# Taking the embedding's product out of the gate: two hybrid decoder layers on one Trainium2 core

## The chip, the core and the metric

The kernel runs on one core of a Trainium2 chip. The core has TensorE (PE, with its weight loads PEld), VectorE (DVE), ScalarE (ACT), GpSimd (POOL) and SyncE (SP, which issues most DMAs). TensorE reads from SBUF and writes to PSUM, which has eight banks of 128 x 512 f32. The metric is device microseconds of one execution: the median over runs of the same program. All inputs, weights and outputs lie in DRAM when an execution begins and ends.

## The reference

Two layers, 512 tokens, width 1024. All arithmetic is f32.

```python
def hybrid_layer(x, p_i, positions, w_in, ...):
    h = x @ w_in                                  # q, k, v of two head groups, and an indexer
    oa = swa_sink_attention(qa, ka, va, sinks)    # window of 128 keys, with sinks
    ob = dsa_sparse_attention(qb, kb, vb, qi, ki, wi, k_top)   # 128 best keys by the indexer's score
    mix = jnp.concatenate([oa, ob], axis=-1) @ w_o
    x = layer_norm(DN_ALPHA * x + mix, ln1_g, ln1_b)
    g, u = jnp.split(x @ w_gu, 2, axis=-1)
    ffn = (jax.nn.silu(g) * u) @ w_down
    ple = (p_i @ w_pp) * jax.nn.sigmoid(x @ w_pg)
    return layer_norm(DN_ALPHA * x + ffn + ple, ln2_g, ln2_b)
```

The change is about `ple`. Its factor `p_i @ w_pp` (512 x 256 by 256 x 1024) depends on two inputs of the kernel alone, and not on `x`; it is called the embedding's product below. The other factor, `sigmoid(x @ w_pg)`, is the gate.

## The kernel before

The tokens lie in four tiles of 128 (`t` = 0 to 3); `xt[t]` holds the residual stream of one tile. For products the stream is turned to features by `to_features` (line 406) into `fh` and `fl`, the high and the low part of each value. Every product of that kind is three matmuls, `mm3` (line 314): high by high, high by low, low by high. The matmuls of nearly all products therefore bear the lines 316 to 318, and they are told apart by their tiles.

A weight goes through a queue written out ahead (`wq`, line 163, filled by `plan`). `w_dma` loads a block of 512 KB into one of three staging buffers `wst` by SP; `w_split` turns it into a high part (ACT, line 269) and a low part (POOL, line 270) in one of five buffers `wsp`. A block marked `extra` goes to `slot` buffers instead, by ACT (line 263) and DVE (line 264). `w_take` hands a block to a product, `w_rel` gives the buffer back and starts the next split. There are 28 buffers `slot` and 12 buffers `t2k` of 128 x 512. All PSUM tiles come from one pool of eight banks.

The stages of a layer, in the order of the program:

- `start()` (line 791): `project` multiplies tile by tile with the indexer's columns, 296 wide (`gi_out`, line 518, normalizes and rotates the indexer's keys and queries on DVE, with parts on ACT and POOL; its `turns` transpose them later), then with the keys' and values' columns, 384 wide (`kv_out`, line 559), in two blocks of two tiles, then the first queries.
- `index()` (line 610) runs interleaved with it, by the costs that a small planner (`Order`, line 42) adds up: for `t` = 1 to 3 it waits until the turned keys and queries are there, and then issues eight score matmuls (line 617) of 128 to 512 columns, each with a relu on ACT (line 619) and a weighted sum on DVE (line 620). `topk()` (line 625) follows on DVE.
- `rest()`, `attention()` and `topk()` interleaved; then `last_o()` (line 822), the last part of the output projection, by single tiles. The norm behind the attention, `ln_sums` (line 395), starts for a tile when its last half is there; DVE does most of it (lines 402 and 404).
- `gate_up(True, ...)` (line 831) begins the feed-forward part: `to_features(0)`, `to_features(1)`, products of the first 256 tokens, `to_features(2)`, `to_features(3)`. The feed-forward part is six groups (`GROUPS`, line 178). In the group after the first, `p` (loaded in line 959) is transposed in lines 947 to 955 and kept as `pT` in four `slot` buffers.
- The gate (lines 979 to 1020): for each of the four tiles and each half `h` of the 1024 columns, 24 matmuls of 512 columns with `w_pg` into the bank `ps`, then six with `w_pp` into the bank `pq` (line 997). ACT takes the sigmoid of `ps` (line 1002), DVE multiplies by `pq` (line 1003) and adds to the stream (line 1012, in the second layer 1005), and the second norm follows. The blocks of the second half are `extra`. At the end of the first layer `to_features` and the next `start()` follow; at the end of the second the output is stored.

Tile builds each engine's queue from the program. It keeps the order of what depends on one another, but may issue later work earlier on an engine where an earlier instruction is not ready by its own model of time.

## Time and profile before

| | us |
|---|---|
| time, median of 3 runs (1295.0 to 1297.23) | 1295.97 |
| profiled execution, its own time | 1295.42 |
| its span in the trace | 1293.6 |
| PE busy | 1244.4 (96%) |
| DVE busy | 837.7 (65%) |
| POOL busy | 666.8 (52%) |
| ACT busy | 575.7 (44%) |

The page gives busy time by engine, the span in 40 slices, the DMA queues and the chain of work that ended last: 81% of that chain is PE's, 12% DVE's. The stages lie so in the span: first layer to 653.7 us (indexer and attention to 241.9, feed-forward part to 596.8, gate to 653.7), second layer behind it (attention to 873.5, feed-forward part to 1228.5, gate to 1283.4, the last norm and store to 1293.6). The timelines and the table by stretches show each engine in such a stage; a matmul's duration there is modelled and overlaps the next one's, so that start to start is the measure of its cost.

### The profile page before, as it was taken

How to read it: one execution, taken by the hardware profiler on the slowest of the kernel's cores; microseconds unless marked ns; L12 is line 12 of the kernel's file. 1: busy time of each engine (PE TensorE's matmuls, PEld its weight loads, DVE VectorE, ACT ScalarE, POOL GpSimd, SP SyncE). 2: the span in 40 equal slices, each digit the busy share in tenths (PEclk: the TensorE clock that was granted, in tenths of full speed). 3: DMA queues.
4: the chain of work that ended last, by engine and by line, in shares of the span. 5: the costliest groups of instructions: out<-in, count | busy, mean ns of one | idle time of the engine just before them, and what ended most of it. 6: DMA issues, size and time to landing. Idle time of an engine off the chain costs nothing.

```text
span 1293.6 us, 18329 instructions
## 1 busy us (share of the span) xinstructions
PE 1244.4 (96%) x6632; PEld 1073.3 (83%) x6632; DVE 837.7 (65%) x1866; ACT 575.7 (44%) x1216; POOL 666.8 (52%) x477
## 2 busy tenths in 40 slices
PE   6799999899999999999998999998999999999996
PEld 4799889788888888888897997888888888888885
DVE  8899965864545453635679997765827273636276
ACT  2656765343343433333337576744434343434220
POOL 7565432357475757563155544414665665757422
PEclk9799999999999999999998999999999999999998
DMA  5133121332232424134032313103342414231321
GB/s 171 50 98 99 58 74 33 98 109 92 94 114 82 129 67 131 33 114 136 2 97 70 111 34 98 50 17 128 101 126 70 139 59 145 67 113 34 114 82 49
DMA packets 89123, 112.77 MB, mean 87 GB/s; under 512 B 5444, under 2 KB 65860, under 8 KB 89032
## 3 DMA queue, kind: packets, MB, share of 16 engines
q1 hardware_dynamic: 88360, 111.58, 27.8%
q8 instruction: 52, 0.85, 0.3%
q14 instruction: 39, 0.32, 0.1%
q10 hardware_dynamic: 672, 0.03, 0.0%
HBM read 109.49 MB, written 2.10 MB: 86 GB/s over the span
## 4 chain that ended last, share of the span: by engine, by line
PE 81%; DVE 12%; ACT 2%; issue 2%; DMA 1%; POOL 1%; DVEq 0%; SPq 0%; POOLq 0%; ACTq 0%
PE bank L316 24%; PE bank L317 24%; PE bank L318 24%; PE bank L656 2%; PE bank L700 2%; DVE t2k L476 2%; PE bank L694 2%; DVE work L620 1%; DVE m L631 1%; DVE work L632 1%; DVE t2k L474 1%; DMA wst<-in_w_pg_dram 1%; DVE x L404 1%; POOL wsp L270 1%; PE bank L486 1%
## 5 line engine op out<-in xcount | busy, mean ns | idle before, releaser
L270 POOL TENSOR_TENSOR wsp<-wst,wsp 128x1024 fp32r<-128x1024 f32 (+2 forms) x148 | 353.4, 2402 | 273.4 <-ACT wsp L269 271.2
L317 PE MATMUL bank<-fl,wsp 128*128 128x512 f32 (+1 forms) x768 | 284.9, 372 | 2.0 <-DVE fl L415 2.0
L316 PE MATMUL bank<-fh,wsp 128*128 128x512 f32 (+1 forms) x768 | 283.6, 372 | 1.0 <-ACT fh L414 1.0
L318 PE MATMUL bank<-fh,wsp 128*128 128x512 f32 (+1 forms) x768 | 283.2, 371 | 0.0
L269 ACT CAST wsp<-wst 128x1024 fp32r<-128x1024 f32 (+2 forms) x148 | 151.3, 1032 | 158.3 <-PE bank L318 108.1
L843 DVE TENSOR_TENSOR t2k<-bank,t2k 128x512 f32<-128x512 f32 x44 | 30.4, 692 | 222.2 <-PE bank L318 222.2
L317 PEld LDWEIGHTS bank<-fl,wsp 128*128 128x128 f32 x768 | 144.7, 188 | 27.4 <-DVE fl L415 2.4
L316 PE MATMUL bank<-wsp,fh 128*128 128x256 f32 (+3 forms) x512 | 165.9, 326 | 0.7 <-ACT fh L414 0.3
L318 PE MATMUL bank<-wsp,fl 128*128 128x256 f32 (+3 forms) x512 | 164.6, 323 | 1.5 <-DVE fl L415 1.5
L316 PEld LDWEIGHTS bank<-fh,wsp 128*128 128x128 f32 x768 | 143.6, 188 | 26.6 <-ACT fh L414 1.9
L318 PEld LDWEIGHTS bank<-fh,wsp 128*128 128x128 f32 x768 | 144.7, 188 | 24.9
L317 PE MATMUL bank<-wsp,fh 128*128 128x256 f32 (+3 forms) x512 | 164.4, 321 | 0.0
L248 POOL TENSOR_TENSOR wsp<-slot,wsp 128x512 fp32r<-128x512 f32 x100 | 141.5, 1439 | 28.5 <-ACT wsp L247 28.5
L316 PE MATMUL bank<-wsp,slot 128*128 128x512 f32 x392 | 153.5, 392 | 0.0
L317 PE MATMUL bank<-wsp,slot 128*128 128x512 f32 x392 | 152.7, 390 | 0.0
L775 DVE TENSOR_TENSOR x<-bank,x 128x512 f32<-128x512 f32 x140 | 91.5, 686 | 88.5 <-PE bank L318 88.5
L318 PE MATMUL bank<-wsp,slot 128*128 128x512 f32 x392 | 148.4, 389 | 0.0
L875 ACT CAST slot<-t2k 128x256 fp32r<-128x256 f32 (+1 forms) x104 | 49.8, 497 | 144.1 <-DVE t2k L843 102.5
L248 POOL TENSOR_TENSOR wsp<-t2k,wsp 128x512 fp32r<-128x512 f32 x40 | 57.5, 1448 | 93.0 <-ACT wsp L247 93.0
L316 PEld LDWEIGHTS bank<-wsp,fh 128*128 128x128 f32 x512 | 98.3, 192 | 7.5 <-ACT fh L414 1.0
L318 PEld LDWEIGHTS bank<-wsp,fl 128*128 128x128 f32 x512 | 97.9, 192 | 7.1 <-DVE fl L415 2.1
L317 PEld LDWEIGHTS bank<-wsp,fh 128*128 128x128 f32 x512 | 98.4, 192 | 5.4
(166 smaller groups left out, 2189.4 us busy)
## 6 DMA issues: line engine op xcount, KB each, us to landing
wst<-in_w_gu_dram SPq DMA_DIRECT2D x88, 512.0 KB, 3.5
slot<-in_w_down_dram SPq DMA_DIRECT2D x80, 256.0 KB, 2.8
wst<-in_w_in_dram SPq DMA_DIRECT2D x16, 512.0 KB, 3.6
wst<-in_w_o_dram SPq DMA_DIRECT2D x16, 512.0 KB, 3.7
wst<-in_w_pg_dram SPq DMA_DIRECT2D x16, 512.0 KB, 4.0
wst<-in_w_in_dram SPq DMA_DIRECT2D x8, 256.0 KB, 2.8
lng<-in_ln_g_dram SPq DMA_DIRECT2D x4, 512.0 KB, 6.3
lnb<-in_ln_b_dram SPq DMA_DIRECT2D x4, 512.0 KB, 6.3
```

Of the source, the lines that this page charges most:

```text
L248: G.tensor_tensor(w[:, 1, j], src[j], w[:, 0, j], OP.subtract)
L269: A.copy(w[:, 0, :a * n], st[:, :a * n])
L270: G.tensor_tensor(w[:, 1, :a * n], st[:, :a * n], w[:, 0, :a * n], OP.subtract)
L316: PE.matmul(o, sh, mh, start=start, stop=False, skip_group_check=again)
L317: PE.matmul(o, sh, ml, start=False, stop=False, skip_group_check=again)
L318: PE.matmul(o, sl, mh, start=False, stop=stop, skip_group_check=again)
L476: V.tensor_tensor(t1.rearrange("p n (u i) -> p n u i", u=2), t1.rearrange("p n (u i) -> p n u i", u=2), t2.rearrange("p n (u i) -> p n u i ...
L656: PE.matmul(ps[:, o:o + nn], qT[kind, t, g][:, j * 128:(j + 1) * 128], kT[c, s][:, k0:k0 + nn], start=(s == 0), stop=(s == 1))
L694: PE.matmul(o, vt[b0 + b][:, f:f + 128], pts[b][:, u], start=b == 0 and u == 0, stop=b == nb - 1 and u == 1)
L775: V.tensor_tensor(xt[t][:, c], ps, xt[t][:, c], OP.add)
L843: V.tensor_tensor(a, ps[1, f], a, OP.mult)
L875: A.copy(h[0], src)
```

## The change

The embedding's product leaves the gate. Its first half of columns is computed in `index()`, ahead of the first score matmuls of tile 1; the second half in the first `gate_up`, two tiles behind `to_features(0)` and two behind `to_features(1)`. `p` is no longer loaded into `slot` buffers: a new entry of the weight queue, "stage", loads it into a staging buffer (512 KB), twice a layer, and `embed_parts` transposes and splits it, twice a layer, into four `t2k` buffers. `embed` makes six matmuls for a tile, ACT copies the bank to a `t2k` buffer and issues a DMA that writes it to a tile in DRAM. `w_pp` takes a `wsp` buffer each time, between the keys' weights and the queries', and between the output projection's and the feed-forward part's. In the gate, SP loads the eight pieces back (256 KB each) into `slot` buffers, and the multiplication of line 1003 reads them there and not in PSUM.

```diff
--- before.py
+++ after.py
@@ -97,6 +97,7 @@
     slots = ctx.enter_context(tc.tile_pool(name="slots", bufs=NSLOT))
     tmp = ctx.enter_context(tc.tile_pool(name="tmp", bufs=NTMP))
     small = ctx.enter_context(tc.tile_pool(name="small", bufs=4))
+    dram = ctx.enter_context(tc.tile_pool(name="dram", bufs=1, space=bass.MemoryType.DRAM))
     psum = ctx.enter_context(tc.tile_pool(name="psum", bufs=1, space=bass.MemoryType.PSUM))
 
     order = Order()
@@ -169,6 +170,11 @@
     def rows(w, k, a, c0, c1):
         return w[k * 128:(k + a) * 128, c0:c1]
 
+    def plan_embed(l, h):
+
+        wq.append(("stage", (p[l, 0],), None))
+        plan(2, rows(w_pp[l], 0, 2, h * 512, (h + 1) * 512))
+
     def plan_down(w, f):
 
         wq.append(("raw", w, f))
@@ -181,6 +187,7 @@
             plan(a, rows(w_in[l], k, a, QI, NIN))
         for k in range(0, KT, 2):
             plan(2, rows(w_in[l], k, 2, KA, KA + 256), rows(w_in[l], k, 2, KB, KB + 128))
+        plan_embed(l, 0)
         for c in (QA, QA + 256, QB, QB + 256):
             for k in range(0, KT, 4):
                 plan(4, rows(w_in[l], k, 4, c, c + 256))
@@ -188,6 +195,7 @@
             for h in range(2):
                 for k in range(k0, k0 + 4, 2):
                     plan(2, rows(w_o[l], k, 2, h * 512, (h + 1) * 512))
+        plan_embed(l, 1)
         for fs in GROUPS:
             for f in fs:
                 for c in (f * 256, FF + f * 256):
@@ -201,7 +209,6 @@
         for h in range(2):
             for k in range(0, KT, 2):
                 plan(2, rows(w_pg[l], k, 2, h * 512, (h + 1) * 512), extra=h == 1)
-            plan(2, rows(w_pp[l], 0, 2, h * 512, (h + 1) * 512), extra=h == 1)
 
     wst_live, w_live = {}, {}
     W_AHEAD, ST_AHEAD = 5, 3
@@ -223,6 +230,7 @@
                     SP.dma_start(quarter[q][j], w[r:r + 128, h * 512:(h + 1) * 512])
             return
         a, cols, _ = wq[i]
+        a = 4 if a == "stage" else a
         n = sum(ap.shape[1] for ap in cols)
         st = wst.tile([128, 1024], F32, name="wst", tag="wst")
         sv = st[:, :a * n].rearrange("p (a n) -> p a n", a=a)
@@ -236,7 +244,7 @@
 
     def w_split(i):
 
-        if wq[i][0] == "raw":
+        if wq[i][0] in ("raw", "stage"):
             return
         if wq[i][0] == "op":
             src = quarter[wq[i][1]]
@@ -292,7 +300,7 @@
                 wpos["dma"] += 1
                 go = True
             i = wpos["split"]
-            if i < wpos["dma"] and (wpos["room"] or wq[i][0] == "raw" or wq[i][2] is True and wq[i][0] != "op"):
+            if i < wpos["dma"] and (wpos["room"] or wq[i][0] in ("raw", "stage") or wq[i][2] is True and wq[i][0] != "op"):
                 w_split(i)
                 wpos["split"] += 1
                 go = True
@@ -306,6 +314,12 @@
         wpos["use"] = i + 1
         assert i in w_live, (i, wpos)
         return w_live.pop(i)
+
+    def stage_take():
+        i = wpos["use"]
+        wpos["use"] += 1
+        assert wq[i][0] == "stage" and i < wpos["split"], i
+        return wst_live.pop(i)
 
     def w_rel():
         wpos["room"] += 1
@@ -514,6 +528,7 @@
         qiT, qT, work, wi, vt, vb, ma = {}, {}, {}, {}, {}, {}, {}
         ready = set()
         kin, kmv = {}, {}
+        pe, first_half = {}, []
 
         def gi_out(t, ps):
 
@@ -607,9 +622,36 @@
                 yield None
 
 
+        def embed_parts():
+            st = stage_take()
+            parts = []
+            for k in range(2):
+                ps = bank("tp", 2)
+                for t in range(NT):
+                    PE.transpose(ps[:, tok(t)], st[:, t * 256 + k * 128:t * 256 + (k + 1) * 128], idf)
+                parts.append([t2k(F32R), t2k(F32R)])
+                A.copy(parts[k][0], ps)
+                V.tensor_tensor(parts[k][1], ps, parts[k][0], OP.subtract)
+            return parts
+
+        def embed(t, h, parts, w):
+            ps = acc()
+            for k in range(2):
+                mm3(ps, parts[k][0][:, tok(t)], parts[k][1][:, tok(t)], w[0][k], w[1][k], k == 0, k == 1)
+            a = t2k()
+            A.copy(a, ps)
+            pe[t, h] = dram.tile([128, 512], F32, name=f"pe{t}{h}", tag=f"pe{t}{h}")
+            A.dma_start(pe[t, h], a)
+
+
         def index():
             for t in range(1, NT):
                 yield from wait(("i", t), *[("ki", b) for b in range(0, t + 1, 2)])
+                if t == 1:
+                    for u in range(NT):
+                        embed(u, 0, *first_half)
+                    w_rel()
+                    yield 5.4
                 nk = (t + 1) * 128
                 work[t] = const.tile([128, nk], F32, name=f"work{t}", tag=f"work{t}")
                 for h in range(IH):
@@ -798,6 +840,7 @@
                     ln_in(t + 1)
                 yield from project(ws, 296, (t,), from_f, gi_out, 3 * (t == 3))
             ws = take(4)
+            first_half.extend([embed_parts(), w_take()])
             for b in ALL:
                 yield from project(ws, 384, b, from_f, kv_out, 4 * (b is ALL[-1]))
             for q in QS[:NSTART]:
@@ -818,6 +861,7 @@
         order.run((rest(), R_MAIN), (attention(), 1.0), (topk(), R_TOP))
         order.flush()
         wo = [take(2), take(2)]
+        second_half = embed_parts(), w_take()
 
         def last_o():
             for b in TAIL:
@@ -845,7 +889,12 @@
 
             if first:
                 to_features(0)
+                for t in range(2):
+                    embed(t, 1, *second_half)
                 to_features(1)
+                for t in range(2, NT):
+                    embed(t, 1, *second_half)
+                w_rel()
                 for j in range(2):
                     ps[j, 0], ps[j, 1] = acc(), acc()
                     for k in range(KT):
@@ -943,21 +992,6 @@
                         w_sums(hs[0]["end"])
                 else:
                     gate_up(False, lambda f, a: hs.append(parts(a)[0]))
-                if gi == 1 and f == fs[0]:
-                    pT = {}
-                    for k in range(2):
-                        ps = bank("tp", 2)
-                        for t in range(NT):
-                            o = t % 2 * 256 + k * 128
-                            PE.transpose(ps[:, tok(t)], pin[t // 2][:, o:o + 128], idf)
-                        pT[k] = [slot(), slot()]
-                        A.copy(pT[k][0], ps)
-                        V.tensor_tensor(pT[k][1], ps, pT[k][0], OP.subtract)
-            if gi == 0:
-                pin = [slot(F32), slot(F32)]
-                for i in range(2):
-                    SP.dma_start(pin[i].rearrange("p (t n) -> p t n", t=2),
-                                 p[l, 0, i * 256:(i + 1) * 256].rearrange("(t p) n -> p t n", p=128))
             if len(fs) == 2:
                 down(hs, gi == 0)
                 continue
@@ -976,31 +1010,29 @@
                     res_out(h, None)(t, ps[t])
 
 
-        wg = [take(5) if h == 0 else None for h in range(2)]
+        wg = [take(4) if h == 0 else None for h in range(2)]
+        for t in range(NT):
+            for h in range(2):
+                e = slot(F32)
+                SP.dma_start(e, pe[t, h])
+                pe[t, h] = e
         for b in TAIL:
             for h in range(2):
                 if wg[h] is None:
-                    wg[h] = take(5)
+                    wg[h] = take(4)
                 ws = wg[h]
                 c = slice(h * 512, (h + 1) * 512)
                 ps = [acc() for _ in b]
-                pq = [bank("sc", 2) for _ in b]
                 for k in range(KT):
                     w = ws[k // 2]
                     for i, t in enumerate(b):
                         mm3(ps[i], *from_f(t, k), w[0][k % 2], w[1][k % 2], k == 0, k == KT - 1)
                     if b is TAIL[-1] and h == 0 and k % 2 == 1:
                         w_rel()
-                for k in range(2):
-                    w = ws[4]
-                    for i, t in enumerate(b):
-                        mm3(pq[i], pT[k][0][:, tok(t)], pT[k][1][:, tok(t)], w[0][k], w[1][k], k == 0, k == 1)
-                if b is TAIL[-1] and h == 0:
-                    w_rel()
                 for i, t in enumerate(b):
                     a = t2k()
                     A.activation(a, ps[i], AF.Sigmoid)
-                    V.tensor_tensor(a, pq[i], a, OP.mult)
+                    V.tensor_tensor(a, pe[t, h], a, OP.mult)
                     if l == L - 1:
                         V.tensor_tensor(xt[t][:, c], xt[t][:, c], a, OP.add)
                         ln_stats(t, h)
```

## Rows read from the trace of the kernel before

**Rows 1.** By stretch, us: busy PE, PEld, DVE, ACT, POOL (counts), clock, DMA, GB/s

```profile
53.53:66.94 13.41, 12.17 (x44) 9.92 (x45) 11.37 (x34) 10.48 (x32) 3.17 (x8) 0.50 0.01 2
...
105.00:160.00 55.00, 52.94 (x409) 49.97 (x407) 54.49 (x194) 41.37 (x127) 23.81 (x26) 1.00 0.28 86
...
596.80:653.70 56.90, 56.76 (x260) 46.88 (x259) 37.16 (x75) 21.99 (x39) 14.64 (x7) 1.00 0.27 81
...
684.18:691.80 7.62, 7.51 (x32) 6.10 (x32) 5.76 (x14) 6.88 (x20) 1.45 (x5) 0.51 0.02 4
...
691.80:736.00 44.20, 42.47 (x333) 41.80 (x333) 43.72 (x114) 26.07 (x74) 29.06 (x27) 1.00 0.28 84
```

**Rows 2.** PE's matmuls by operands, second layer's gate: count, busy us and mean ns

```profile
L316 PE MATMUL bank<-wsp,slot 128*128 128x512 f32 x8 | 3.1, 389 | 0.0
...
L318 PE MATMUL bank<-slot 128*128 128x512 f32 x8 | 3.1, 389 | 0.0
```

**Rows 3.** Timeline of PE, end of the last gate: start, length us, instruction

```profile
1278.67 0.39 PE L317 MATMUL bank<-slot,fh 128*128 128x512 f32 x1
...
1282.97 0.39 PE L318 MATMUL bank<-slot 128*128 128x512 f32 x1
```

**Rows 4.** Timelines of ACT and DVE at the same place

```profile
1282.04 0.60 ACT L1002 ACTIVATE t2k<-bank 128x512 f32<-128x512 f32 x1 [6.20 <-PE bank L318]
...
1283.47 0.69 DVE L1003 TENSOR_TENSOR t2k<-bank,t2k 128x512 f32<-128x512 f32 x1 [4.35 <-PE bank L318]
```

**Rows 5.** PE ahead of the first scores, both layers; [idle before <- releaser]

```profile
46.81 0.96 PE L486 MATMUL bank<-idr,slot 128*128 128x128 f32 x10
...
53.53 2.73 PE L617 MATMUL bank<-slot 128*128 128x256 f32 x8 [5.75 <-ACT slot L487]
...
684.18 2.73 PE L617 MATMUL bank<-slot 128*128 128x256 f32 x8 [5.89 <-ACT slot L487]
```

**Rows 6.** Timelines of DVE and ACT there, first layer

```profile
52.30 0.42 DVE L474 TENSOR_TENSOR t2k<-bank,tab 128x256 f32<-128x256 f32 x1
...
61.31 0.61 DVE L474 TENSOR_TENSOR t2k<-bank,tab 128x128 f32<-128x128 f32 x2
...
52.42 0.30 ACT L479 CAST slot<-t2k 128x128 fp32r<-128x128 f32 x1 [4.07 <-DVE t2k L476]
...
52.62 1.34 ACT L487 CAST slot<-bank 128x256 fp32r<-128x256 f32 x3
```

**Rows 7.** Timeline of PE at the norm behind the attention, first layer, then second

```profile
243.65 1.09 PE L412 MATMUL bank<-idf,x 128*128 128x128 f32 x8 [1.71 <-DVE x L404]
...
246.48 0.39 PE L317 MATMUL bank<-fl,wsp 128*128 128x256 f32 x1 [0.99 <-DVE fl L415]
...
252.65 1.09 PE L412 MATMUL bank<-idf,x 128*128 128x128 f32 x8 [0.39 <-DVE x L404]
...
875.40 1.09 PE L412 MATMUL bank<-idf,x 128*128 128x128 f32 x8 [1.71 <-DVE x L404]
```

**Rows 8.** Timelines of SP's issues and of PE, first layer's gate

```profile
587.02 0.37 SPq L231 DMA_DIRECT2D wst<-in_w_pp_dram  x1
...
589.74 11.56 SPq L231 DMA_DIRECT2D wst<-in_w_pg_dram  x4
...
608.23 0.50 PE L317 MATMUL bank<-slot,fh 128*128 128x512 f32 x1
```

**Rows 9.** Timeline of DVE, end of the first layer's gate; POOL splits until 653.96

```profile
648.50 0.68 DVE L1003 TENSOR_TENSOR t2k<-bank,t2k 128x512 f32<-128x512 f32 x1
...
649.21 1.25 DVE L1012 CUSTOM_DVE_ANT_0 x<-x,t2k 128x512 f32<-128x512 f32 x1
...
654.44 0.69 DVE L1012 CUSTOM_DVE_ANT_0 x<-x,t2k 128x512 f32<-128x512 f32 x1
```

**Rows 10.** Prices of DMAs: timeline of ACT's queue, then issues by line

```profile
1.18 0.53 ACTq L151 DMA_DIRECT2D invf<-in_inv_freq_dram  x1
...
slot<-in_w_down_dram SPq DMA_DIRECT2D x80, 256.0 KB, 2.8
```

## The prediction

> **What bounds the kernel now.** I read the chain of work that ended last first: four fifths of it are TensorE's. Then the table by stretches, for where PE is not full, and the waits and timelines of those places. In the gate PE is busy for 56.76 of 56.90 us, in the second layer alike, so that a matmul taken from there should shorten the time by what it costs [rows 1]. There are two kinds of places where PE stands still. Ahead of the first score matmuls it waits 5.75 us in the first layer and 5.89 in the second, both times for ACT's copy of the turned keys [rows 5]; behind the pause it runs at half its clock, at a granted clock of 0.50 for 13.41 us and of 0.51 for 7.62 [rows 1]. At the norm behind the attention it waits 1.71, 0.99 and 0.39 us for DVE, together 3.09, and the first of these returns in the second layer at the same size [rows 7]. In the attention itself neither engine has room: from 105 to 160 us DVE is busy for 54.49 of 55 us and PE for 52.94, and from 691.8 to 736 DVE for 43.72 of 44.20 [rows 1]. The sum below is therefore made by stage: gate, first pause, norm.
>
> **The gate.** There are six groups of eight matmuls of the embedding's product for a layer, of which the first and the last are shown; that is 48 a layer [rows 2]. From the start of the matmul at 1278.67 to that at 1282.97 are 4.30 us for 19 matmuls, 0.226 each [rows 3]. 96 of them are 21.7 us that leave a full engine. At the very end a little comes back: the last six matmuls hide the sigmoid. ACT begins it at 1282.04, right behind the last product with w_pg, it takes 0.60, and the multiplication follows only at 1283.47, when the six are through [rows 4]. Without them it could start at about 1282.74, 0.73 earlier, where the six cost 1.36: +0.63. The multiplication keeps its length of 0.69 [rows 4]. In the first layer the next layer's projections stand behind the gate on PE; I count no such end there.
>
> Does PE get its weights that much earlier? Before, the block of w_pp is loaded at 587.02 between the two halves of w_pg, and the four blocks of the second half are issued over 11.56 us from 589.74; only one matmul is held visibly, 0.50 us long instead of 0.39, at 608.23 [rows 8]. PE now comes to the second half 1.36 us earlier, but the block that was loaded in front of it is gone, and each of the four moves up by one staging buffer, which is more than 1.36 us. I take nothing for it. SP gets eight loads of 256 KB behind w_pg's. Such a load takes 2.8 us to land [rows 10], its first reader is DVE behind a whole column of matmuls, and eight banks let PE go on; nothing, unless they are issued in front of w_pg's blocks. Those four took 11.56 us of SP's time for the same number of bytes [rows 8], so that loads in front of them could make them late by as much; I hold at most about 5 us a layer to show. In the feed-forward part two small loads, four slot buffers and the transposes go; the eight transposes return in the output projection's last part, full as well, and the other eight lie in the first pause: net nothing.
>
> **The norm.** Half of the product, 24 matmuls, is 5.43 us a layer. It stands where PE waits 3.09 us; its inputs have been ready long before. The first two tiles' matmuls (2.7 us) begin in the wait of 1.71 [rows 7], and push the next transposes back by about 1; the other two fill the wait of 0.99 and, being late by then, the wait of 0.39. What stays is 5.43 - 3.09 = 2.34 a layer, 4.7 for both. Bounds: nothing of it hidden, 10.9; better than 4.7 only if DVE's part ended earlier, which nothing here makes it do. ACT's four copies and four DMA issues lie beside DVE's chain. w_pp now holds a fifth wsp buffer, so that the first block of the feed-forward part is split about when its neighbours are; it is wanted 5 us later than before.
>
> **The first pause.** The other 5.43 us are as long as the pause of 5.75 or 5.89 [rows 5]. Three things decide how much fits. (1) Banks: each tile wants one of eight. When the ten transposes end (46.81 + 0.96), three banks wait for ACT's three copies at 52.62, and the two of the keys' product are held by DVE, which reads one at 52.30 and one at 61.31 [rows 5, 6]. Three tiles can go at once, 4.1 us; the fourth waits until about 53.1, and the first score follows at about 54.5 and not at 53.53: one microsecond late, for DVE too, which is full from there on. (2) ACT: four copies of about 0.6, by the sigmoid of the same size [rows 4], and four DMA issues, 0.53 by the only kind on ACT's queue [rows 10]: 4.5 us. ACT stands idle for 4.07 us up to 52.42, held by one instruction that waits for DVE [rows 6]; behind it, it is busy for 10.48 of 13.41 us [rows 1]. Copies that are queued behind the held instruction delay scores, those ahead of it cost nothing. (3) The transposed p wants two subtractions on DVE, 1.4 us by the 0.69 of one such read from a bank [rows 4], and four of twelve t2k buffers. Against these stands the clock: without a long pause it may not fall. The half clock can give back no more than what DVE leaves: 13.41 - 11.37 = 2.04 us in the first layer and 7.62 - 5.76 = 1.86 in the second [rows 1]. So the bounds for a layer are -2 and +6.8 (5.43 not hidden, and 1.4 on DVE). I take +1, the late fourth tile, with the clock's gain set against ACT and DVE: +2 for both layers.
>
> The sum: 1293.6 - 21.7 + 0.6 + 4.7 + 2.0 = 1279.2 us of span. The profiled execution took 1.8 us more than its span, and the median of the runs lies 0.55 above that execution: 1281.6, forecast 1281.5.
>
> **Rivals.** First, the moved half stays out of the pause: the block of w_pp comes late, or copies line up on ACT, and both layers pay near 6.8 instead of 1. For it: DVE and ACT are nearly full behind the pause, and a delay there meets DVE's top-k work. Against it: three banks are free. 1281.5 + 11.6 = 1293. Second, the gate does not shrink as the matmuls do, since the loads from DRAM are issued ahead of w_pg's second half: 5 us a layer, 1291.5. Against it: w_pg stands in front in the program. A third runs through DVE. The multiplication reads its factor from a bank now and from SBUF afterwards. At 648.50, while POOL is splitting, line 1003 with one operand in a bank takes 0.68, and line 1012 with both operands in SBUF takes 1.25 at 649.21, against 0.69 at 654.44 with POOL idle [rows 9]. If all sixteen multiplications paid that 0.56 and the chain went through DVE, the time would be 1281.5 + 9 = 1290.5. It doesn't by DVE's load, 37.16 of 56.90 us in the gate [rows 1], so that I give it little. The Trainium skill, page "SBUF — State Buffer", section "Who interferes with whom", has the rule for it: a VectorE instruction with two SBUF inputs contends with a GpSimd instruction that reads SBUF, and one with at most one doesn't. The rows at 648.50 and 649.21 agree with it, and it speaks against this part of the change.
>
> The rival on the other side is slower than before: t2k buffers. Tile may issue work early, and the transposes for the second half depend on nothing but a load. If their four buffers are taken before the attention's last units have theirs, these have eight of twelve. A unit over tile 3 keeps four for its exponentials, and three units are under way at a time, so that from there on one unit less overlaps. PE then waits once for each of the four units of the last two tiles in each layer. The price of one is the pause that a late step leaves, between the 1.71 of a DVE step and the 5.75 of a whole chain [rows 5, 7]; at 3 each it is 8 x 3 = 24 us, 1305. It decides as soon as the parts are made before the last unit's scores; that the output projection's last part precedes them in the program speaks against it.
>
> A better case: the clock stays up, and ACT's hole takes the copies: -2 a layer, 1275.5.
>
> **How the numbers follow.** The forecast with its neighbourhood, 1277 to 1286: 0.56. The first rival, in part or whole, 0.14; the gate's two together 0.11 (the one by DVE 0.03 of it); the better case 0.06; slower by the t2k buffers or the like 0.08; and 0.05 lies between the first rival with an unhidden norm and no change. The range of 8 in 10 goes from 1274.5 to 1292.0: it takes in the better case and most of the first two rivals. 0.2%, 2.6 us, is about what a measurement of this kernel tells from no change: faster by more 0.86, within 0.05, slower by more 0.09.
>
> **What would show it.** In the gate 192 matmuls of w_pg a layer and no others, PE full, the stage 10.9 us shorter in each layer: right. PE waiting for ACT or DVE slots there: the second rival. Ahead of the first scores, 24 matmuls where the pause was, what is left of it under 2 us, a granted clock of 1.00 behind it, and the first score one microsecond later behind the keys' copies. If it is 5 later, or if DVE has new idle time between 53 and 160 us, I was wrong by the first rival. At the norm the first feed-forward products start 2.3 us later than before, seen from the output projection's last matmul. PE idle in the attention's last tiles beside a wait for t2k: the slower rival. The prediction is wrong as a whole if attention, from the first score to the norm, grows by more than the gate gave.

## The result, and the profile after

The changed kernel takes 1304.42 us (median of 4 runs, 1304.17 to 1306.88) where the kernel before takes 1295.79 beside it; the ratio is 1.0070, 95% interval 1.0052 to 1.0087. It is slower by 0.7%, and 23 us above the forecast of 1281.5. One run of those below, of `e17_bank`, took 1355.79 with its core in a slower state, and its median leaves it out.

First the page of the changed kernel: busy time of each engine, and the clock granted to TensorE in 40 slices.

```profile
span 1305.1 us, 18472 instructions
...
PE 1252.3 (96%) x6648; PEld 1082.5 (83%) x6648; DVE 842.4 (65%) x1866; ACT 584.1 (45%) x1234; POOL 673.4 (52%) x479
...
PEclk9999999999999999999997999998999999999998
```

PE has 7.9 us more busy time than before (1244.4), of which the 16 transposes that it makes more are about 1.8, at 0.11 from start to start; the span is 11.5 longer. So some of the loss is slower matmuls, and the rest is waits. The profiled execution of the changed kernel took 1306.88, the longest of its four. 1.8 of that come in the first 31 us and belong to this execution: in `e3_pin`, whose program is the same up to there, they are 0.0.

The next table divides both spans at events that each program has once: the start of PE's transposes (line 412 before, 426 after), of the first feed-forward product over all 512 tokens, and of the first gate product. A change of length is the difference of the two differences.

| stage, up to | before, us | after, us | change of length | forecast |
|---|---|---|---|---|
| start, to tile 2's first transposes | 28.81 | 30.60 | +1.79 | 0 |
| layer 1 attention, to the norm's transposes | 240.90 | 246.61 | +3.92 | +1.0 |
| norm, to the products over 512 tokens | 272.68 | 285.42 | +7.03 | +2.34 |
| feed-forward, to the first gate product | 596.82 | 608.67 | -0.89 | 0 |
| gate, to tile 3's transposes | 664.14 | 670.29 | -5.70 | -10.86 |
| layer 2 attention | 872.65 | 887.75 | +8.95 | +1.0 |
| norm | 904.43 | 927.32 | +7.79 | +2.34 |
| feed-forward | 1228.58 | 1250.57 | -0.90 | 0 |
| gate, norm and store, to the end | 1293.6 | 1305.1 | -10.5 | -10.23 |

The second gate does what was forecast: in its stretch PE is full (columns as in [rows 1]), and by operands it runs 192 matmuls, all with w_pg.

```profile
1250.57:1294.26 43.69, 43.69 (x193) 35.85 (x191) 35.19 (x70) 7.50 (x12) 12.00 (x7) 1.00 0.27 96
```

The first gate gives back half of it. The feed-forward parts are 0.9 shorter by the eight transposes that left them. Both norms and both attentions cost far more than forecast. Now these places, in rows.

Timeline of PE ahead of the first scores, both layers (start, length, instruction, idle time before it and its releaser); these answer to [rows 5].

```profile
48.67 0.97 PE L500 MATMUL bank<-idr,slot 128*128 128x128 f32 x10
...
53.28 0.50 PE L330 MATMUL bank<-wsp,t2k 128*128 128x512 f32 x1 [2.64 <-DVE t2k L634]
...
61.37 0.75 PE L659 MATMUL bank<-slot 128*128 128x256 f32 x5
...
689.67 0.79 PE L332 MATMUL bank<-wsp,t2k 128*128 128x512 f32 x1 [3.44 <-DVE t2k L634]
...
696.95 0.85 PE L659 MATMUL bank<-slot 128*128 128x256 f32 x4
```

The product is in the pause, but it waits there itself, for the low parts of p (line 634). DVE makes them last, behind the whole rotation of the indexer's keys, and ACT's four copies and stores stand ahead of the scores' relus:

```profile
52.55 1.28 DVE L634 TENSOR_TENSOR t2k<-bank,t2k 128x512 fp32r<-128x512 f32 x2
...
63.69 0.48 DVE L662 SCALAR_TENSOR_TENSOR work<-bank,wi,causal 128x256 f32<-128x256 f32 x1 [9.20 <-ACT bank L661]
...
58.10 0.59 ACT L642 COPY t2k<-bank 128x512 f32<-128x512 f32 x1 [1.73 <-PE bank L332]
58.72 0.34 ACTq L644 DMA_DIRECT2D pe<-t2k  x1
...
61.85 0.59 ACT L642 COPY t2k<-bank 128x512 f32<-128x512 f32 x1 [0.77 <-PE bank L659]
62.33 1.05 ACT L277 CAST wsp<-wst 128x1024 fp32r<-128x1024 f32 x1
...
63.28 0.92 ACT L661 ACTIVATE bank<-bank 128x256 f32<-128x256 f32 x3
```

The first score is 7.84 us late (6.05 without the start), and DVE idles 9.20 us. The clock falls all the same: by the table of stretches (columns as in [rows 1]) it is 0.70 from 61.40 to 70.00, and 0.50 for 9 us behind the second layer's first scores.

```profile
700.00:709.00 9.00, 8.18 (x26) 7.24 (x27) 8.11 (x26) 5.81 (x22) 4.30 (x9) 0.50 0.21 58
```

At the norm, timelines of PE, then ACT, then DVE; PE's rows answer to [rows 7].

```profile
250.22 1.04 PE L426 MATMUL bank<-idf,x 128*128 128x128 f32 x8
...
254.77 0.50 PE L330 MATMUL bank<-fh,wsp 128*128 128x256 f32 x2 [0.75 <-ACT fh L428]
258.38 1.09 PE L426 MATMUL bank<-idf,x 128*128 128x128 f32 x8 [3.10 <-DVE x L418]
...
252.24 1.05 ACT L642 COPY t2k<-bank 128x512 f32<-128x512 f32 x2
...
253.18 1.05 ACT L277 CAST wsp<-wst 128x1024 fp32r<-128x1024 f32 x1
...
254.13 1.08 ACT L428 CAST fh<-bank 128x512 fp32r<-128x512 f32 x2
...
255.62 2.70 DVE L418 SCALAR_TENSOR_TENSOR x<-x,lns,lnb 128x1024 f32<-128x1024 f32 x1
258.43 1.27 DVE L429 TENSOR_TENSOR fl<-bank,fh 128x512 fp32r<-128x512 f32 x2
```

The old waits of 1.71 and 0.99 are filled, as forecast. But tile 1's transposes are done at 251.3, and ACT copies their result only at 254.13, behind two copies of the product and a split; DVE's low part of it (258.43) then falls behind a step of the norm. Tile 2's transposes stand behind two feed-forward matmuls on PE, where they stood behind 48: Tile planned them there. PE waits 3.10.

At the end of the first gate, PE, DVE and POOL:

```profile
658.03 1.25 PE L426 MATMUL bank<-idf,x 128*128 128x128 f32 x8 [3.91 <-DVE x L418]
...
650.37 2.20 DVE L1035 TENSOR_TENSOR t2k<-slot,t2k 128x512 f32<-128x512 f32 x1
...
652.61 2.21 DVE L1044 CUSTOM_DVE_ANT_0 x<-x,t2k 128x512 f32<-128x512 f32 x1
...
656.60 1.28 DVE L418 SCALAR_TENSOR_TENSOR x<-x,lns,lnb 128x1024 f32<-128x1024 f32 x1
...
649.19 2.83 POOL L278 TENSOR_TENSOR wsp<-wst,wsp 128x768 fp32r<-128x768 f32 x1
...
651.99 2.28 POOL L278 TENSOR_TENSOR wsp<-wst,wsp 128x768 fp32r<-128x768 f32 x1
```

The wait of 3.91 is new. Tile 3's multiplication and addition, which read SBUF alone, lie in the middle of tile 2's norm, and take 2.2 us each while POOL splits. Each of them ends 0.55 us after the split beside which it began (at 652.57 and 654.82, the splits at 652.02 and 654.27).

### The profile page after: what moved, and what is told of

Its sections match the earlier page's. It is cut to its first block, busy times and chain, and to the rows that moved or that the text cites. A ratio compares the mean times of both kernels' runs of the same rounds, so it can differ in the third digit from the quotient of the medians.

```text
span 1305.1 us, 18472 instructions
## 1 busy us (share of the span) xinstructions
PE 1252.3 (96%) x6648; PEld 1082.5 (83%) x6648; DVE 842.4 (65%) x1866; ACT 584.1 (45%) x1234; POOL 673.4 (52%) x479
## 4 chain that ended last, share of the span: by engine, by line
PE 81%; DVE 13%; ACT 2%; issue 2%; DMA 0%; POOL 0%; DVEq 0%; SPq 0%; ACTq 0%; POOLq 0%
PE bank L332 25%; PE bank L330 25%; PE bank L331 25%; DVE t2k L490 2%; PE bank L698 2%; DVE work L674 2%; PE bank L742 2%; DVE m L673 1%; DVE t2k L488 1%; DVE t2k L701 1%; DVE work L662 1%; PE bank L736 1%; DVE x L418 1%; PE bank L426 1%; PE bank L500 1%
## 5 line engine op out<-in xcount | busy, mean ns | idle before, releaser
L278 POOL TENSOR_TENSOR wsp<-wst,wsp 128x1024 fp32r<-128x1024 f32 (+2 forms) x150 | 359.1, 2408 | 307.5 <-ACT wsp L277 292.7
L330 PE MATMUL bank<-wsp,fh 128*128 128x256 f32 (+3 forms) x512 | 167.9, 331 | 0.3 <-ACT fh L428 0.2
L331 PE MATMUL bank<-wsp,fh 128*128 128x256 f32 (+3 forms) x512 | 167.2, 327 | 0.0
L330 PE MATMUL bank<-wsp,slot 128*128 128x512 f32 x376 | 147.2, 392 | 0.0
L331 PE MATMUL bank<-wsp,slot 128*128 128x512 f32 x376 | 146.3, 389 | 0.0
L332 PE MATMUL bank<-wsp,slot 128*128 128x512 f32 x376 | 142.2, 389 | 0.0
L330 PEld LDWEIGHTS bank<-wsp,fh 128*128 128x128 f32 x512 | 100.5, 197 | 7.0 <-ACT fh L428 0.9
L331 PEld LDWEIGHTS bank<-wsp,fh 128*128 128x128 f32 x512 | 100.6, 196 | 5.3
```

Source lines behind the costliest of these rows:

```text
L278: G.tensor_tensor(w[:, 1, :a * n], st[:, :a * n], w[:, 0, :a * n], OP.subtract)
L330: PE.matmul(o, sh, mh, start=start, stop=False, skip_group_check=again)
L331: PE.matmul(o, sh, ml, start=False, stop=False, skip_group_check=again)
L332: PE.matmul(o, sl, mh, start=False, stop=stop, skip_group_check=again)
```

## The experiments

"Attention", "norm" and "gate" below are changes of the table's lengths against before, in the profiled executions. They scatter: the attentions are +3.92 and +8.95 in the changed kernel, +3.54 and +4.88 in `e3_pin` and +1.69 and +8.69 in `e17_bank`, whose programs differ from it elsewhere only. The start differs by up to 2.8 us, and a norm that nothing changed by up to 1.9 (the second layer's in `e1_first` and `e15_parts`). Of the edits the main lines are shown, with dots for what is left out. Times are medians, ratios are against runs of the kernel before on the same chip.

### One half at a time

**First half alone:** the second half's product goes back into the gate, with its weights and transposes.

```diff
-        plan_embed(l, 1)
...
-        second_half = embed_parts(), w_take()
...
-                    embed(t, 1, *second_half)
```

> Only the first half of the columns is moved (ahead of the first scores); the second half stays in the gate as before, so 48 matmuls leave it, 10.9 us by 0.226 each. Theory (the place ahead of the scores costs more than the gate gives: in the trace of after, the first score matmul is 7.8 us late in the first layer, and the transposes behind the attention's norm are 5.7 late there and another 9 to 10 later in the second layer): 1297 to 1301. Rival (this place is nearly free, as I had forecast, 2 us for both layers, and the loss is all at the norm): 1287 to 1288.

1293.67, ratio 0.9974 (0.9961 to 0.9988): faster than before. Attention is +2.37 and +4.27, the gates -5.87 and -5.79. The theory's sign was wrong: this half gains; but the place costs three times the forecast and more.

**Second half alone:** the same edit for the other half.

```diff
-        plan_embed(l, 0)
...
-                        embed(u, 0, *first_half)
...
-            first_half.extend([embed_parts(), w_take()])
```

> Only the second half is moved (to the norm behind the attention); the first stays in the gate. 10.9 us leave the gate. Theory (from the norm's first transposes to the steady feed-forward products the trace of after is 7.0 us longer in the first layer and about 7.8 in the second, because tile 2's transposes are queued ahead of ready products and PE waits 3.10 us for DVE, with half clock behind it): 1296 + 14.8 - 10.9, so 1297 to 1302. Rival (the norm costs what I had forecast, 4.7 for both layers): 1289 to 1291.

1303.77, ratio 1.0054 (1.0039 to 1.0069). Norms +7.02 and +7.00, gates -3.43 and -5.22. So most of the loss is at the norm, and the first gate's end is a third place.

### The norm

**Transposes in place:** those of tiles 2 and 3 are held on PE behind the product that precedes them.

```diff
-                            product(j, f, k, slice(0, 256))
-                    to_features(2 + j)
+                            last = product(j, f, k, slice(0, 256))
+                    with tc.issue_after(last.ins):
+                        to_features(2 + j)
```

> The changed kernel with one thing added: the transposes of tiles 2 and 3 in the first feed-forward block are held on PE behind the product that precedes them in the program, as they stood before. Theory (Tile's order put tile 2's transposes ahead of 46 ready products; 3.10 us of wait and about 1.8 of half clock a layer come from that): PE's wait of 3.10 gone, the granted clock 1.00 there, 1294 to 1298. Rival (the wait is DVE's norm and only moves to a later place): 1302 to 1305.

1302.89, ratio 1.0049 (1.0033 to 1.0065). The theory falls: norms +7.81 and +8.06. PE now waits at the next matmul, for the low part of tile 1:

```profile
252.59 0.51 PE L330 MATMUL bank<-fh,wsp 128*128 128x256 f32 x2 [0.73 <-ACT fh L428]
256.98 0.58 PE L331 MATMUL bank<-fl,wsp 128*128 128x256 f32 x1 [3.88 <-DVE fl L429]
```

The order on PE was a symptom. What is late are tile 1's features.

**ACT's order too:** on `e2_second`, with `e3_pin`'s edit, the product's copies (now in `embed_store`) are held behind ACT's copies of tile 1.

```diff
-                    embed(t, 1, *second_half)
-                to_features(1)
-                for t in range(2, NT):
-                    embed(t, 1, *second_half)
+                held = [embed(t, 1, *second_half, False) for t in range(2)]
+                end = to_features(1)
+                held += [embed(t, 1, *second_half, False) for t in range(2, NT)]
+                with tc.issue_after(end.ins):
+                    for t in range(NT):
+                        embed_store(t, 1, held[t])
```

> The second half alone is moved, as in e2_second (1303.77), and the order at the norm is mended: ACT's four copies of the product are held behind its copies of tile 1's features, and the transposes of tiles 2 and 3 stay behind the products that precede them. Theory (in e2_second and e3_pin, ACT copies tile 1's features only behind two copies of the product, two squares and a weight split, DVE's low parts then stand behind tile 2's and tile 3's norm, and PE waits 3.1 to 3.9 us and falls to half clock): PE's wait there under 1.5 us, no half clock, from the norm's first transposes to the steady products at most 4 us more than before instead of 7, time 1294 to 1298. Rival (the matmuls themselves cost it, since nothing of the norm hides them): 1301 to 1304.

1298.38, ratio 1.0006 (0.9994 to 1.0018), 5.4 less than `e2_second`. Norms +4.72 and +3.22. Timelines of PE and ACT, and a stretch with its clock:

```profile
251.53 0.39 PE L332 MATMUL bank<-fl,wsp 128*128 128x256 f32 x1 [1.72 <-DVE fl L430]
...
248.68 1.06 ACT L429 CAST fh<-bank 128x512 fp32r<-128x512 f32 x2
249.63 1.07 ACT L649 COPY t2k<-bank 128x512 f32<-128x512 f32 x2
...
252.00:256.00 4.00, 4.00 (x23) 4.00 (x22) 3.79 (x9) 1.18 (x2) 3.43 (x2) 0.59 1.06 380
```

ACT's copies stood in the way. The time is just above what was expected: 1.72 of the wait stays, since DVE still takes a step of tile 3's norm first, and against the theory the clock falls behind it, to 0.59 for 4 us. In the second layer, with a wait of 1.73, it stays at 1.00; that is the difference between the two norms. This run changes PE's order and ACT's; `e3_pin` shows that PE's alone gains nothing at the norm, and ACT's alone was not run.

### The pause

**Behind tile 1's scores:** `if t == 1` becomes `if t == 2` in `index()`.

> The changed kernel with the first half's product one step later: behind the scores of tile 1 and ahead of those of tile 2. Theory (the loss is that the first scores, and with them DVE's weighted sums and top-k, start 7.8 us later): the first score matmul is back within 1 to 2 us of before, DVE's idle time of 9.2 us ahead of its first weighted sum falls to 2 to 3, and the time is 1293 to 1299. Rival (PE is full behind the pause, so that 24 matmuls cost their length wherever they stand, and only the waits inside them go): 1300 to 1304.

1305.72, ratio 1.0075 (1.0058 to 1.0092). The first score comes at 54.83; less 2.83 that this execution is late at the start, that is 1.5 us earlier than before [rows 5]. The attention is +5.64 and +6.48. The two sum to 12.1, where the changed kernel has 12.9, and the times can't be told apart: the early first score did not help, and behind the scores there is no more room than ahead of them. The rival was right, even low.

**One matmul of six:** on `e1_first`, so that 20 matmuls a layer less stand in the pause, and all else is there.

```diff
-            for k in range(2):
-                mm3(ps, parts[k][0][:, tok(t)], parts[k][1][:, tok(t)], w[0][k], w[1][k], k == 0, k == 1)
+            PE.matmul(ps, parts[0][0][:, tok(t)], w[0][0], start=True, stop=True)
```

> As e1_first, with one matmul instead of six for each tile of the moved half (that part of the embedding's product is left out); its loads, splits, transposes, copies and stores stay. 40 matmuls of 0.226, 9.0 us of full clock, are gone from the two pauses. Theory (the pause holds part of the matmuls, and the rest is paid at PE's price): e1_first costs 3.1 and 3.9 us at the attention's end, so 1293.7 less 6 to 7, 1286 to 1289. Rival (the price is that of the parts around them: DVE's subtractions, ACT's copies and stores, one buffer of weights): 1291 to 1294.

1288.04, 5.6 less than `e1_first` for 9.0 us of matmuls. I took it for a price of the matmuls. The runs below show that it depends on the queues around them: `e16_evict1` gains 7.3 with all matmuls there.

**p split earlier:** on `e1_first`, p is loaded behind the indexer's weights and transposed ahead of tile 2.

```diff
+                if t == 2:
+                    first_half.append(embed_parts())
                 yield from project(ws, 296, (t,), from_f, gi_out, 3 * (t == 3))
```

> The first half alone is moved, as in e1_first (1293.67), but p is transposed and split earlier, ahead of the indexer's product for tile 2, so that DVE's subtractions no longer stand behind the indexer's norm and rotations. Theory (the matmuls wait 2.6 us in the first layer and 3.4 in the second for these subtractions and run at half clock behind them): both waits gone, first scores 3 to 5 us earlier than in e1_first, of which the attention keeps about half: 1288 to 1291. Rival (the score matmuls wait for ACT's copies of the keys and for DVE in any case, and the product only fills time): 1293 to 1295.

1292.45, ratio 0.9958 (0.9941 to 0.9976): 1.2 less, with intervals that overlap. The wait of 2.6 for DVE is gone and the first score comes 4 us sooner (3.2 without the starts), but the attention is +3.65 and +3.32, no better than `e1_first` beyond scatter.

**Copies on DVE, in the changed kernel:** DVE copies the first half's banks, SP issues the stores.

```diff
-            A.copy(a, ps)
+            (V.tensor_copy if h == 0 else A.copy)(a, ps)
...
-            A.dma_start(pe[t, h], a)
+            (SP if h == 0 else A).dma_start(pe[t, h], a)
```

> The changed kernel (1304.42) with one thing changed: the first half's four copies ahead of the first scores are made by DVE and stored by SP instead of ACT. Theory (ACT's queue makes the pause dear; e14_dve against e11_share gave 5.7): 5 to 7 less, 1297 to 1300. Rival (in the changed kernel DVE's subtractions of p stand late, and the copies, now behind the same chain on DVE, gain nothing): 1303 to 1306.

1302.94, ratio 1.0051 (1.0036 to 1.0066): 1.5 less, with intervals that overlap, so alone this gives as little.

**Both together,** and nothing else changed in the changed kernel:

> The changed kernel (1304.42) with both changes of the pause and none elsewhere: p transposed ahead of the indexer's product for tile 2 (as in e7_early) and the first half's copies on DVE, stored by SP (as in e19_dve, 1302.94). Theory (the product in the pause is held first by DVE's late subtractions and then by ACT's queue; with one of them left the other gives nothing, with both gone the pause holds the product): the attention's norm at most 1 us later than before, apart from the start, instead of 4 to 6, 1294 to 1298. Rival (what e14_dve gained came from its other orders, the shared parts above all): 1300 to 1303.

1289.12, ratio 0.9941 (0.9924 to 0.9957): 15.3 less than the changed kernel, and 5 below the theory's range. Attention +0.30 and +1.95, with the second half's transposes still in it: the pause now holds the product. The norms are untouched at +7.64 and +7.81. Timeline of ACT:

```profile
53.69 1.34 ACT L502 CAST slot<-bank 128x256 fp32r<-128x256 f32 x3
55.85 1.06 ACT L278 CAST wsp<-wst 128x1024 fp32r<-128x1024 f32 x1 [0.82 <-issue]
56.81 1.06 ACT L502 CAST slot<-bank 128x512 fp32r<-128x512 f32 x2
57.76 2.33 ACT L662 ACTIVATE bank<-bank 128x256 f32<-128x256 f32 x8
```

The relus begin at 57.76; in `e7_early`, where ACT has the four copies, at 60.42; in the changed kernel at 63.28, of which 1.8 are the start. Between the two profiled spans lie 15.4 us: 10.6 are the attentions, 3.7 the first gate (-9.37 where it was -5.70), to which I come below, and 1.75 the starts; the norms take 0.6 back. The first score still comes at 56.24, 2.7 later than before, and a bank holds the fourth tile for 1.15.

### All places together

**Norm and pause mended,** the copies of the pause still on ACT: the edits of `e6_late` and `e7_early` in the changed kernel.

> Both halves moved, as in the changed kernel (1304.42), with the orders of e6_late (ACT's copies of the product behind tile 1's features, transposes of tiles 2 and 3 in place) and of e7_early (p transposed ahead of tile 2's product). Theory (the losses are separate and add): 5.4 by e6_late against e2_second and 1.2 by e7_early against e1_first come off: 1296 to 1299. Rival (Tile's order is another for every program, and one mended place is lost at the next): 1301 to 1304.

1289.25, ratio 0.9946 (0.9928 to 0.9964), 7 us better than the theory's best. Norms +3.22 and +3.24, attention +4.46 and +6.24, gate -9.24: it has the first gate's 3.5 as well, which I had not counted.

**p split once a layer,** on top of that; its four parts stay in slot buffers through the attention.

```diff
-        second_half = embed_parts(), w_take()
+        second_half = first_half[0], w_take()
```

> As e10_both, with p loaded, transposed and split once a layer and not twice: the second half uses the first half's four parts, which stay in slot buffers through the attention. Theory (where the second half alone was moved, the output projection's last part begins 2.2 to 3.4 us late in each layer, before any matmul of the product: eight transposes of 0.15 on PE and two subtractions of 0.69 on DVE in a stage where both are full): 4 to 6 us less than e10_both, 1291 to 1294. Rival (four of 28 slot buffers are missed in the attention, or the delay has another cause): same as e10_both or more.

1288.35, ratio 0.9934 (0.9916 to 0.9951). The intervals overlap: the theory's 4 to 6 did not come, and the second transposing is not shown to cost anything.

**The second transposing by itself,** in the kernel before, unused:

```diff
         wo = [take(2), take(2)]
+        embed_parts()
```

> The kernel before with one thing added and not used: a second load of p, its eight transposes, two copies on ACT and two subtractions on DVE ahead of the output projection's last part, in both layers. Forecast (nothing, the stage's queues hide it): 1296 to 1297. Theory (the stage is full on PE and DVE; where the second half alone was moved it ended 2.2 to 3.4 us late): 1300 to 1303, the output projection's last part 2 to 3 us late in each layer.

1299.48, ratio 1.0009 (0.9995 to 1.0023). The median lies between the two expectations; by the interval it is nothing that can be told from zero, and under 3 us. Nothing here speaks against that forecast, net nothing.

**ACT relieved in the pause:** on `e11_share`, with the edit of `e19_dve`.

> As e11_share (1288.35), with the four copies ahead of the first scores made by DVE and their stores issued by SP, so that nothing of the product is queued on ACT there. Theory (ACT's copies and issues, 4 x 0.59 and 4 x 0.33, stand ahead of the scores' relus and the keys' copies, and PE waits 2 to 4 us a layer for these in the attention's first 15 us): 2 to 6 us less, 1283 to 1286. Rival (the stage is bound by PE's sum of matmuls, and DVE is as full as ACT): 1288 or more, up to 1293 by DVE's four copies of 0.69 a layer.

1282.66, ratio 0.9886 (0.9866 to 0.9906), 5.7 less than `e11_share`, and the best version: 1.1% below the kernel before.

**Copies left out:** on `e11_share`, only tile 0's copy and store are kept.

```diff
+            if h == 0 and t > 0:
+                pe[t, h] = pe[0, h]
+                return
```

> As e11_share, with the copies and stores of three of the four tiles left out ahead of the first scores (the gate then reads the first tile's piece for all four: that part of the output is left out). The 24 matmuls stay. Theory (queue of ACT): 2 to 6 us less than e11_share, 1283 to 1286. Rival (the matmuls themselves are what the pause cannot hold): 1287 to 1289.

1281.00, ratio 0.9881 (0.9853 to 0.9908). With all 24 matmuls there, 7.3 us go with three copies and stores: ACT's queue is the price, and moving the copies to DVE is worth nearly as much as leaving them out.

### The first gate's end

**The sigmoid stays in its bank,** in the changed kernel, so that the multiplication has one operand in SBUF.

```diff
-                    A.activation(a, ps[i], AF.Sigmoid)
-                    V.tensor_tensor(a, pe[t, h], a, OP.mult)
+                    A.activation(ps[i], ps[i], AF.Sigmoid)
+                    V.tensor_tensor(a, pe[t, h], ps[i], OP.mult)
```

> The changed kernel with the sigmoid left in its bank, so that DVE's multiplication reads one operand from PSUM again and only one from SBUF. Theory (two SBUF operands beside POOL's splits made that multiplication 2.20 us instead of 0.69 in the middle of tile 2's norm at the first gate's end): that row returns to about 0.69, the addition behind it stays near 2.2, PE's wait of 3.91 falls to about 2.4, the time by about 1.5: 1301 to 1304. Rival (the length comes from something else): row and wait unchanged.

1299.22, ratio 1.0021 (1.0009 to 1.0032). Timelines of PE, DVE and POOL:

```profile
651.77 1.09 PE L426 MATMUL bank<-idf,x 128*128 128x128 f32 x8 [1.59 <-DVE x L418]
...
646.43 0.67 DVE L1035 TENSOR_TENSOR t2k<-slot,bank 128x512 f32<-128x512 f32 x1
...
647.13 1.51 DVE L1044 CUSTOM_DVE_ANT_0 x<-x,t2k 128x512 f32<-128x512 f32 x1
...
645.24 2.85 POOL L278 TENSOR_TENSOR wsp<-wst,wsp 128x768 fp32r<-128x768 f32 x1
```

With POOL as busy as before the multiplication takes 0.67 again, the wait falls to 1.59, the gate is -9.53. The addition, with both operands in SBUF still, ends at 648.64, again 0.55 after the split. The theory holds, though the gain is above its range; the whole run gained 5.2, of which the gate's 3.8 show where. The kernels with p split early show the other side: there p, which is not split, is the fourth block of the next layer, and POOL has a gap just then. From `e20_pause`, DVE and POOL:

```profile
645.61 0.68 DVE L1038 TENSOR_TENSOR t2k<-slot,t2k 128x512 f32<-128x512 f32 x1
646.32 0.69 DVE L1047 CUSTOM_DVE_ANT_0 x<-x,t2k 128x512 f32<-128x512 f32 x1
...
640.95 3.53 POOL L279 TENSOR_TENSOR wsp<-wst,wsp 128x888 fp32r<-128x888 f32 x2 [26.88 <-ACT wsp L278]
647.21 1.84 POOL L279 TENSOR_TENSOR wsp<-wst,wsp 128x768 fp32r<-128x768 f32 x1 [2.73 <-ACT wsp L278]
```

Same instructions, both operands in SBUF, 0.68 and 0.69 with POOL idle, and PE's wait is 0.91.

**DVE's order there:** on `e11_share`, tile 3's multiplications are held behind tile 2's norm.

```diff
-                    V.tensor_tensor(a, pe[t, h], a, OP.mult)
+                    with tc.issue_after(normed.ins) if l < L - 1 and t == 3 else nullcontext():
+                        V.tensor_tensor(a, pe[t, h], a, OP.mult)
```

> As e11_share, with one order more: at the end of the first layer, DVE's multiplications of tile 3 are held behind the last step of tile 2's norm. Theory (PE's wait of 3.91 us ahead of tile 2's transposes, new in the changed kernel, comes from two instructions of tile 3 of 2.2 us each that DVE takes in the middle of that norm): the wait falls under 1 us and the time by 2 to 4 against e11_share. Rival (the norm of a tile is longer than the shorter gate of the next tile hides, whatever stands between): wait and time stay within 1 us.

1295.42, ratio 0.9991 (0.9981 to 1.0001), 7 more than `e11_share`. The wait was 0.90 by then already, so that there was nothing to win; it is 0.85 now, and 1.95 more come at tile 3. That is 2.1 of the 7; 1.5 more are at the first norm, behind which the clock fell here. The second attention is +6.40 where `e11_share` has +1.90; why stays open.

**The bank on top of the best version:** `e14_dve` with the edit of `e17_bank`.

> As e14_dve (1282.66), with the sigmoid left in its bank as in e17_bank, so that the multiplication reads one operand from SBUF. Theory (these instructions stand in tile 2's norm at the first gate's end, where PE now waits 0.88 us; elsewhere DVE has room): 0.5 to 1.5 less, 1281 to 1282.5. Rival (the bank is held longer, until DVE has read it, and PE waits for banks in the gate): 1283 to 1286.

1284.05, ratio 0.9905 (0.9889 to 0.9922): no gain over `e14_dve`, as the intervals overlap. The wait was 0.88 before and is 0.83.

## Why the prediction was wrong

**The gate on PE: right.** The second layer's gate to the end is 10.5 us shorter, forecast 10.23 with the sigmoid's end. Weights and loads from DRAM never held PE there; the rival of late weights did not come about.

**The first gate's end: the step that failed** is "I count no such end there". The shorter gate of tile 3 no longer covers tile 2's norm, and that norm had grown. I had the mechanism, as the rival of DVE's multiplication from SBUF, and dismissed it by an average, DVE's 37.16 of 56.90 us [rows 1]. It needed one chain, not a full engine. Its size was off too, since one row was taken for the price: such an instruction ends 0.55 us after the split beside which it began, and the 1.25 us of [rows 9] began 0.7 before a split's end, the 2.20 and 2.21 each 1.65 before. The Trainium skill, page "SBUF — State Buffer", section "Who interferes with whom", says that a VectorE instruction with two SBUF inputs contends with a GpSimd instruction that reads SBUF, and one with at most one, outside the two-port modes, does not; 2.20 against 0.67 in `e17_bank` agrees. PE's wait was 3.91; the two instructions account for 3.0 of it, at 0.69 each, and `e20_pause` has 0.91. Of the time about 3.7 went there by `e20_pause`'s gate; the other 1.3 to 1.5 against the forecast stay in `e17_bank`, `e20_pause` and `e14_dve` alike.

**The norm: the step that failed** is "ACT's four copies and four DMA issues lie beside DVE's chain". Its arithmetic of PE was right: 5.43 less the filled waits. But ACT's copies of tile 1's features are part of the chain to the first products, and the moved copies got ahead of them. 2.34 a layer became 7.03 and 7.79. With the order mended 3.2 a layer stay where the clock holds and 4.7 where it falls (`e6_late`, `e10_both`), so that my figure was 0.9 low as well; a wait of 1.72 by DVE's order is in both.

**The pause: the step that failed** is the choice of +1 between -2 and +6.8. Of the conditions that I named, banks were not the limit; the other two failed. I had written that copies ahead of the held instruction "cost nothing"; ACT's copies came behind it, since the product was late; and it was late because DVE's two subtractions, which I had counted as 1.4 us of work and not by their place in the queue, came last. The clock fell again. My first rival, "copies line up on ACT", is what happened, at 0.14, and the sign that I had set for it came: a first score 6.05 us late and 9.20 us of new idle time on DVE. In the table it is +3.92 and +8.95 against +1 each, with the scatter told above. `e7_early` and `e19_dve` take one cause away each and gain little, and `e10_both`, with p split early and the copies on ACT, still has attentions of +4.46 and +6.24; `e20_pause` takes both and the pause holds the product, as the forecast said it could.

**The sum.** Attention +10.9 over forecast, norms +10.1, first gate +5.2, start +1.8, the rest -2.1 (feed-forward and the last stage): 25.9, which is 1305.1 less the 1279.2 of the forecast's span. The test that I had set for being wrong as a whole, an attention that grows from the first score to the norm by more than the gate gives, was not met: it takes 185.24 us where it took 187.37 in the first layer, and 190.80 where it took 188.47 in the second. The loss lies ahead of the first score and at the norm, but for these 2.3 us of the second layer. The slower rival, t2k buffers, played no part, so that its 1305 beside the measured 1304.42 is luck: in the attention, from 43 us behind the first score on, PE's waits add up to 2.8 us in the first layer and 4.0 in the second, where they were 2.3 and 4.6. `e14_dve`, with the orders as I had assumed them, takes 1282.66, near the forecast of 1281.5, but by partly other terms, and so by luck in part: norms at +4.71 and +3.22, attention at -0.45 and +3.17, the first gate at -9.40 (from its profiled execution, which took 1286.46).

**Open:** the 2 to 4 us by which the second layer's attention differs between programs that are alike there, and the 4.5 us of the second attention in `e13_all`.

## What to carry to other kernels

Moving matmuls into a pause of PE moves their copies, splits and stores into the queues of other engines; cost them by what stands behind them in each queue and whom that keeps waiting, not by the engine's busy share. Where two causes hold one stage, take both away in one run before calling either harmless. An operand that moves from PSUM to SBUF changes the price of its reader where POOL works in SBUF beside it, and one such reader in a chain that PE waits for is enough.

## What the runs showed of the hardware

A DVE instruction of 128x512 f32 with both operands in SBUF took 0.69 us alone. Where it began while POOL ran a subtraction or multiplication with both operands in SBUF, it ended 0.55 us after that one's end, however much of it was left: in the changed kernel's trace 40 began so, took 0.79 to 2.62 us, and all ended 0.546 to 0.552 after. The same holds for the addition of [rows 9], which ended at 650.46, beside this split of the kernel before:

```profile
647.46 2.46 POOL L270 TENSOR_TENSOR wsp<-wst,wsp 128x592 fp32r<-128x592 f32 x1
```

The 206 that read a bank and began beside POOL took 0.67 to 0.74. So the price of such an instruction is not a factor but what is left of POOL's when it begins. The norm's steps pay it too: in `e6_late` one of 1024 columns took 2.65 us at 247.86, where such a step takes 1.28 alone, ahead of the low part for which PE still waits 1.72. No run moved the split that it stands beside.

A wait of PE can cost more than itself. Timeline of PE in `e3_pin`, and the clock granted behind that wait:

```profile
257.36 0.41 PE L332 MATMUL bank<-fh,wsp 128*128 128x256 f32 x1
257.57 0.41 PE L331 MATMUL bank<-fl,wsp 128*128 128x256 f32 x1
...
260.48 0.28 PE L330 MATMUL bank<-fh,wsp 128*128 128x256 f32 x1
260.60 0.28 PE L331 MATMUL bank<-fl,wsp 128*128 128x256 f32 x1
...
256.98:260.48 3.50, 3.50 (x16) 3.50 (x17) 2.92 (x7) 0.00 (x0) 1.38 (x1) 0.52 0.94 322
```

Behind the wait of 3.88 a matmul of 256 columns goes at 0.21 us from start to start, the lower level of 1.2 GHz, and at 0.12 again from 260.5 on: 3.4 us at half speed, of which I estimate 1.7 as lost. That is one fall. A shorter wait at the same place brought one in some executions and not in others. In the seven programs with `e6_late`'s orders PE waits 1.72 to 1.75 us there in both layers; over the 4 us behind it the clock was 0.57 to 0.63 in five of these fourteen places and 1.00 in nine. Beside the fall the norm is +4.71 to +4.73, without it +3.22 to +3.24, so that a fall costs 1.5 us here. From `e6_late`'s second layer, the wait and the clock behind it:

```profile
887.61 0.39 PE L332 MATMUL bank<-fl,wsp 128*128 128x256 f32 x1 [1.73 <-DVE fl L430]
...
888.00:892.00 4.00, 4.00 (x35) 4.00 (x35) 3.79 (x9) 1.26 (x2) 3.43 (x2) 1.00 1.01 367
```

In the kernel before the clock held behind the waits of 1.71 and 0.99 [rows 7]; in the second layer of `e15_parts`, whose norm is the same, it was 0.75 from 874.00 to 880.00 beside waits of 1.71 and 1.00, and that norm took 1.88 longer.
